# Reads of the rotated keys moved from SyncE's to GpSimd's DMA queue, and a sum of squares moved from GpSimd to VectorE

## The chip, the cores and the metric

The kernel runs on one core of a Trainium2 chip. The metric is device time in microseconds (us); the time before is the median of three runs, 2591.28 us (2590.07 to 2592.25). Engines are called as in the profile: PE is TensorE's matmul, PEld its weight load, DVE VectorE, ACT ScalarE, POOL GpSimd, SP SyncE. A trailing q (SPq, ACTq, POOLq) means the engine's instruction queue, from which DMAs are issued.

## The reference

One encoder layer is applied to a prompt of 512 tokens and a sample of 256, with model width 2048, in float32:

```python
h = rmsnorm(x, ln_mix_g); z = h @ w_in        # columns: fourier 1024 | q 1024 | k 256 | v 256
of = fourier_mix(zf, w_fourier)               # 2-D DFT per group of 128 channels, a 128x128 map
q, k = apply_rope(q), apply_rope(k)           # 16 query heads, 4 key heads, head_dim 64
oa = window_attention(q, k, v, attn_sink)     # +-128 tokens, blocks of 128 queries, a sink logit
x = x + concat(rmsnorm(of), rmsnorm(oa)) @ w_out
x = x + square(relu(rmsnorm(x) @ w_up)) @ w_down     # 8192 wide
y = rmsnorm(x, ln_final_g)
```

## The kernel before, in words

Both requests are handled as one block of T = 768 tokens, six row tiles of 128. Each float32 operand of a product is split in a high part (ACT copies it to the matmul type) and a low part (DVE subtracts), and a product is the sum of three matmuls: high by high, high by low, low by high.

The stages are: row norms, transposes of x and the values (to about 57 us); the Fourier columns of `w_in` by a seven-product scheme (`product7`, L256, to 174 us); the remaining columns of `w_in`, with the Fourier groups and the rotation beside them (L788 to L824, 174 to 378 us); attention together with the first half of the output projection (L1065 to L1080, 378 to about 584 us); the second half with the first residual (L1415 to L1426, to 731 us); the up projection (L1193, to 1665 us); the down projection (L1628, to the end). PE's instructions run in the order of the code all through.

**The columns stage.** `n_in` = 20 pieces, each 1024 rows of `w_in` by 256 columns; four pieces make a column pair. The order of pairs is `cols` (L747): the keys (columns 2048 on), then the queries of groups 2, 0, 1 and 3. Each piece is loaded on SP (`piece_load`, L763, by `wload`, L77, into two `raw` buffers), split by ACT (L69) and DVE (L70), and multiplied on PE (L802). Halfway through and at the end of a pair's fourth piece ACT copies the finished half out of PSUM into the tile `zs` (L815). Pairs 0 and 1 go to DRAM and are read again by `load_z` (L678); pairs 2 to 4 keep their tile, and pairs 2 and 3 use the same single buffer (`z_tile`, L674).

The rotation of a pair is done in three parts of 256 tokens. `cross` (L687) multiplies the swapped halves by the sine on POOL; `turned` (L694, L696) multiplies by the cosine and adds on DVE; `parts` makes the high part on ACT (L706 for keys, L709 for queries) and the low part in place on DVE (L707, L710), and stores both to DRAM on ACT's DMA queue (L704): `kh` and `kl` for keys, `qh` and `ql` for queries. A query's high part lies in one of two `qs` buffers until its store has landed; the low part lies in `zs`.

**The reads that the change moves.** `load_k(i)`, i = 0 to 3, reads the rotated keys back into SBUF in the layout of the score product: 0 and 1 read the high parts into the lower and upper 64 partitions of `kdh`, 2 and 3 the low parts into those of `kdl` (L719). In DRAM the rows are ordered (d h), so that each of 64 partitions takes four rows of 768 floats that lie one after another. Each read moves 768 KB.

What runs beside the products is registered with `after(piece, fn)` (L734) and called when the code reaches that piece (L820 to L824). `load_k(i)` is registered at 14.5 + i (L755), `cross` of the pairs 0, 2, 3, 1 at 10.5, 11.5, 15, 16.5 and half a piece later. Up to piece 18 this order of calls isn't the order on the engines: the framework's scheduler orders SP, ACT, DVE and POOL itself. From piece 19 to the end of attention all engines keep the order of the code (L791).

**Attention** (L1004 to L1080). There are 24 units, six query blocks by four key groups. `load_q` (L730) reads a unit's queries on SP; `qk` (L848) makes the scores, first with `kdl`, then with `kdh`; `row_max` (L863, DVE), `exps` (L878, ACT), `normalize` (L893, POOL), `trans` (L905, PE), the split of the transposed weights (L908, L909) and `pv` (L924) follow. Each call stands in a list of events with a due time in units of the output projection's steps (`at`, `later`, L992 to L997), and `run_events` (L999) emits what is due after each step of `proj_slot` (L1038).

**The squares that the change moves.** `load_oa(m)` (L956) reads a finished row tile of attention outputs from DRAM (L965) in two halves of 128x512, splits them for the projection, and then makes the sums of squares for the group norm: `squares` has ACT square both halves in place (L972) and POOL add one to the other (L973); `reduce` (L976, DVE) sums over the four columns of blocks into `sr`. The two calls are 1.2 steps apart (`t_sq` 6.7, `t_red` 7.9, L989). It is called for m = 0 to 4 in attention, between 463 and 586 us, and for m = 5 in the second half of the projection, at 609 us, where it uses buffers of another tile (`cx`). `row_factors` (L1364) turns `sr` into the factor by a matmul with ones (L1367) and a power on POOL (L101).

Of the kernel before, what the change touches and what calls it, by code (L numbers as in the profile page):

```python
# [15 lines left out]
ALU = mybir.AluOpType  # L16
# [15 lines left out]
NKV = 4  # L32
# [8 lines left out]
def hybrid_encoder(ctx: ExitStack, tc: tile.TileContext, a: dict):  # L41
    nc = tc.nc
    ctx.enter_context(tc.manual_schedule(engines={mybir.EngineType.PE}))

    def f32(ap):
        return ap.bitcast(F32)
# [19 lines left out]
    def split(hi, lo, src, scale=None):  # L66

        if scale is None:
            nc.scalar.activation(hi, src, AF.Copy)  # L69
            nc.vector.tensor_tensor(out=lo, in0=src, in1=f32(hi), op=ALU.subtract)  # L70
        else:
            nc.scalar.activation(hi, src, AF.Copy, scale=scale)
            nc.vector.scalar_tensor_tensor(
                out=lo, in0=src, scalar=scale, in1=f32(hi), op0=ALU.mult, op1=ALU.subtract
            )
# [41 lines left out]
    kr_d = [dpool.tile([2 * P, T], F32, tag=f"k{c}", name=f"k{c}") for c in "hl"]  # L117
# [35 lines left out]
    raws = {}  # L153
# [44 lines left out]
    with ExitStack() as ph:  # L198
# [456 lines left out]
        kt = {}  # L655
# [60 lines left out]

        def load_k(i):
            h = slice(i % 2 * HD, (i % 2 + 1) * HD)
            nc.sync.dma_start(f32(kt["kdh" if i < 2 else "kdl"][h]), kr_d[i // 2][:].rearrange("(d h) t -> d h t", h=NKV))  # L719

        units = [(b, g) for b in range(NM) for g in range(NKV)]
        state = {}
# [32 lines left out]
        for i in range(4):  # L755
            after(14.5 + i, lambda i=i: load_k(i))
# [72 lines left out]
    op = out_ctx.enter_context(tc.tile_pool(name="op", bufs=1, reuse_waits="tile"))  # L829
# [3 lines left out]
    mask, sink, kdh, kdl = (kt[c] for c in ("mask", "sink", "kdh", "kdl"))  # L833
# [116 lines left out]
    def oa_tiles(m):  # L950

        oa[m] = [
            op.tile([P, 8, P], F32R, tag=f"of{c}{m - 1}", name=f"oa{c}{m}") for c in "hl"
        ] + [op.tile([P, P], F32, tag=f"sr{m}", name="sr")]

    def load_oa(m, when=lambda dt, fn: fn(), spare=None):  # L956

        oa_tiles(m)
        oh, ol, sr = oa[m]
        if spare is None:  # L960
            raws = [op.tile([P, 4, P], F32, tag="oar", name="oar", bufs=2)[:] for _ in range(2)]
        else:
            raws = spare
        for i, raw in enumerate(raws):
            nc.sync.dma_start(raw, oa_d[m][i * 512 : (i + 1) * 512, :].rearrange("(k p) t -> p k t", p=P))  # L965

        def parts_of(i):
            split(oh[:, 4 * i : 4 * i + 4, :], ol[:, 4 * i : 4 * i + 4, :], raws[i])

        def squares():  # L970
            for raw in raws:
                nc.scalar.activation(raw, raw, AF.Square)  # L972
            nc.gpsimd.tensor_tensor(out=raws[1], in0=raws[1], in1=raws[0], op=ALU.add)  # L973

        def reduce():
            nc.vector.tensor_reduce(out=sr[:], in_=raws[1].rearrange("p k t -> p t k"), op=ALU.add, axis=AX.X)  # L976

        when(t_oa0, lambda: parts_of(0))
        when(t_oa1, lambda: parts_of(1))
        when(max(t_sq, t_oa0, t_oa1), squares)  # L980
        when(max(t_red, t_sq, t_oa0, t_oa1), reduce)
# [22 lines left out]
    for u in range(len(units)):  # L1004
        t = pace * u + t_first
# [806 lines left out]
```

## Time and profile before

| what | value |
|---|---|
| time, median of 3 runs | 2591.28 us (2590.07 to 2592.25) |
| the profiled execution's own time | 2589.57 us |
| its span in the trace | 2587.7 us |
| granted TensorE clock | 0.999 |
| busy: PE, DVE, ACT, POOL | 2576.2, 1812.2, 1124.0, 257.8 us |
| DMA: mean rate over the span | 188 GB/s |
| DMA share of 16 engines: SP's queue, ACT's, POOL's | 39.3%, 11.7%, 5.8% |
| `load_k`, four issues on SP | at 324.14, 333.58, 339.67, 344.04 us |
| first use of `kdl` and `kdh` on PE | 378.0 us |
| L973 on POOL, six of them | 1.28 to 1.29 us each |

All rows but the first are of one profiled execution. Its time is the span plus 1.9 us around it. Times within the trace are microseconds from the start of the span. [...] In the rows of the timeline, the brackets hold the idle time of the engine just before the instruction and what ended it; "sem" waits of a queue aren't counted as busy.

### The profile page before, as it was taken

The page shows a single profiled execution, that of the slowest core. Times are in us where ns is not written, and L with a number is a line of the kernel's source. Part 1 is how long each engine was busy: PE and PEld are TensorE (multiplying, and loading weights), DVE is VectorE, ACT ScalarE, POOL GpSimd, SP SyncE. Part 2 cuts the span into 40 slices and gives each one's busy share as a digit, 9 for nine tenths or more (in the row PEclk, how much of TensorE's full clock was granted, in tenths as well). Part 3 has the DMA queues.
Part 4 walks back from the last instruction along what each step waited for, and adds up shares of the span by engine and source line. Part 5 has one row for each costly group of instructions (what it writes and reads, how often), then busy time and mean ns, then how long its engine had stood idle before and what let it go on. Part 6 is the DMA issues. An engine that isn't in the chain of part 4 may idle for free.

```text
span 2587.7 us, 34958 instructions
## 1 busy us (share of the span) xinstructions
PE 2576.2 (100%) x13580; PEld 2358.4 (91%) x13580; DVE 1812.2 (70%) x2216; ACT 1124.0 (43%) x1574; POOL 257.8 (10%) x359
## 2 busy tenths in 40 slices
PE   9999999999999999999999999999999999999998
PEld 9999998888899999999999999988888888888887
DVE  7966568777555656555877877667776765777687
ACT  6545437674333333333444544433333333333335
POOL 1001332233201011000000000110000000000000
PEclk9999999999999999999999999999999999999999
DMA  7963385345664445456666666675543662555364
GB/s 252 311 226 113 127 240 181 117 135 193 223 193 157 163 160 186 161 190 238 213 214 232 229 215 208 248 301 178 182 156 111 220 232 82 179 179 164 96 209 155
DMA packets 268999, 489.55 MB, mean 189 GB/s; under 512 B 19568, under 2 KB 164000, under 8 KB 267424
## 3 DMA queue, kind: packets, MB, share of 16 engines
q1 hardware_dynamic: 197328, 321.26, 39.3%
q10 hardware_dynamic: 58688, 115.18, 11.7%
q0 software_dynamic: 12816, 50.87, 5.8%
q8 instruction: 107, 1.75, 0.3%
q14 instruction: 60, 0.49, 0.1%
HBM read 360.35 MB, written 126.88 MB: 188 GB/s over the span
## 4 chain that ended last, share of the span: by engine, by line
PE 98%; DVE 1%; DMA 1%; issue 0%; ACT 0%; DVEq 0%; SPq 0%; POOLq 0%; POOL 0%; ACTq 0%
PE pu L1193 36%; PE pd L1628 35%; PE pm L1046 9%; PE pz L802 6%; PE p L268 5%; PE pv L391 1%; PE o L924 1%; PE s L848 1%; PE t L905 1%; PE pe L630 0%; PE pa L609 0%; PE ptx L137 0%; DMA raw<-in_w_in 0%; PE pt L137 0%; DMA qs<-ql 0%; PE pz L630 0%
## 5 line engine op out<-in xcount | busy, mean ns | idle before, releaser
L1193 PE MATMUL pu<-xf,wh 128*128 128x384 f32 x3072 | 780.1, 334 | 0.0
L1193 PEld LDWEIGHTS pu<-xf,wh 128*128 128x128 f32 x3072 | 554.0, 188 | 1.5 <-ACT o L1211 1.1
L1628 PE MATMUL pd<-wl,sh 128*128 128x512 f32 x1332 | 517.8, 389 | 0.0
L1628 PE MATMUL pd<-wh,sh 128*128 128x512 f32 x1332 | 517.8, 389 | 0.0
L1628 PE MATMUL pd<-wh,sl 128*128 128x512 f32 x1332 | 517.6, 389 | 0.0
L1193 PE MATMUL pu<-xf,wl 128*128 128x384 f32 x1536 | 513.2, 334 | 0.0
L1605 ACT ACTIVATE wh<-rd 128x1024 fp32r<-128x1024 f32 x200 | 202.4, 1054 | 522.2 <-PE pd L1628 421.8
L1615 DVE TENSOR_TENSOR wl<-rd,wh 128x1024 fp32r<-128x1024 f32 x200 | 236.1, 1221 | 226.3 <-ACT wh L1605 225.5
L1173 ACT ACTIVATE wh<-ur 128x1024 fp32r<-128x1024 f32 x160 | 170.0, 1063 | 382.7 <-PE pu L1193 216.8
L1628 PEld LDWEIGHTS pd<-wh,sh 128*128 128x128 f32 x1332 | 250.0, 188 | 51.9
L1628 PEld LDWEIGHTS pd<-wl,sh 128*128 128x128 f32 x1332 | 250.0, 188 | 51.9
L1628 PEld LDWEIGHTS pd<-wh,sl 128*128 128x128 f32 x1332 | 249.9, 188 | 51.8 <-DVE sl L1616 0.3
L1193 PEld LDWEIGHTS pu<-xf,wl 128*128 128x128 f32 x1536 | 288.3, 188 | 0.0
L1179 DVE TENSOR_TENSOR wl<-ur,wh 128x1024 fp32r<-128x1024 f32 x160 | 195.4, 1221 | 75.4 <-ACT wh L1173 75.4
L1214 DVE TENSOR_TENSOR o<-pu,o 128x768 f32<-128x768 f32 x160 | 152.8, 955 | 123.3 <-PE pu L1193 115.1
L1598 DVE TENSOR_TENSOR rd<-rd 128x1024 f32<-128x1024 f32 x112 | 131.7, 1217 | 0.0
L1193 PE MATMUL pu<-xs,wh 128*128 128x384 f32 x512 | 129.8, 334 | 0.0
L1173 ACT ACTIVATE wh<-sx 128x1024 fp32r<-128x1024 f32 x64 | 67.9, 1062 | 130.4 <-PE pu L1193 101.9
L268 PE MATMUL p<-xs,wh 128*128 128x384 f32 x448 | 113.8, 334 | 0.0
L1616 DVE TENSOR_TENSOR sl<-sr,sh 128x768 fp32r<-128x768 f32 x111 | 105.5, 950 | 0.0
L1179 DVE TENSOR_TENSOR wl<-sx,wh 128x1024 fp32r<-128x1024 f32 x64 | 78.1, 1222 | 24.1 <-ACT wh L1173 23.9
L1193 PEld LDWEIGHTS pu<-xs,wh 128*128 128x128 f32 x512 | 92.4, 188 | 0.0
(279 smaller groups left out, 3921.9 us busy)
## 6 DMA issues: line engine op xcount, KB each, us to landing
rd<-in_w_down SPq DMA_DIRECT2D x176, 512.0 KB, 5.2
ur<-in_w_up SPq DMA_DIRECT2D x128, 512.0 KB, 3.9
sr<-sd SPq DMA_DIRECT2D x95, 384.0 KB, 5.4
pd<-o ACTq DMA_DIRECT2D x60, 384.0 KB, 2.3
o<-pd POOLq DMA_DIRECT2D x60, 384.0 KB, 6.0
sd<-sm ACTq DMA_DIRECT2D x60, 384.0 KB, 2.8
raw<-in_w_in SPq DMA_DIRECT2D x38, 512.0 KB, 6.0
raw<-in_w_out SPq DMA_DIRECT2D x32, 512.0 KB, 4.5
```

What stands on the lines that cost most here:

```text
L268: nc.tensor.matmul(ps7[bank, g, r][:, :HALF], l[:, i, r * P : (r + 1) * P], x[:, o, 4 * e + i, :], start=(opens and e == 0 and i == 0 and ...
L802: nc.tensor.matmul(ps[c][s][:, :HALF], w[:, i, cs], whole[j // 2][s][o][:, 4 * (j % 2) + i, :], start=first and n == 0, stop=stop and n == 2,)
L1046: nc.tensor.matmul(ps, l(k), w[:, k % 2, :], start=(k == 0 and n == 0), stop=(k == 7 and n == 2))
L1173: nc.scalar.activation(wh[:], raw[:], AF.Copy)
L1179: nc.vector.tensor_tensor(out=wl[:], in0=raw[:], in1=f32(wh[:]), op=ALU.subtract)
L1193: nc.tensor.matmul(ps[:, t, :HALF], w[:, i, t * P : (t + 1) * P], xb[:, o, i, :], start=(s == first_of[bank] and i == 0 and n == 0), stop= ...
L1214: nc.vector.tensor_tensor(out=o, in0=src, in1=o, op=ALU.add)
L1598: add = lambda x, y, op: nc.vector.tensor_tensor(out=x[:], in0=x[:], in1=y[:], op=op)
L1605: nc.scalar.activation(wh[:], t[:], AF.Copy)
L1615: nc.vector.tensor_tensor(out=wl[:], in0=t[:], in1=f32(wh[:]), op=ALU.subtract)
L1616: nc.vector.tensor_tensor(out=sl[:], in0=sr[:], in1=f32(sh[:]), op=ALU.subtract)
L1628: nc.tensor.matmul(o, l[:, q, ts], w[:, ns], start=(j == j0 and (q, t) == (0, 0)), stop=(j == j1 and (q, t) == (1, 2)),)
```

## The change

The four reads of rotated keys are issued by POOL instead of SP, at the same places of the code. The sum of the two squared halves is made by DVE instead of POOL, at the same due time. Buffers, layouts, due times and arithmetic stay as they are.

```diff
         def load_k(i):
             h = slice(i % 2 * HD, (i % 2 + 1) * HD)
-            nc.sync.dma_start(f32(kt["kdh" if i < 2 else "kdl"][h]), kr_d[i // 2][:].rearrange("(d h) t -> d h t", h=NKV))
+            nc.gpsimd.dma_start(f32(kt["kdh" if i < 2 else "kdl"][h]), kr_d[i // 2][:].rearrange("(d h) t -> d h t", h=NKV))
...
         def squares():
             for raw in raws:
                 nc.scalar.activation(raw, raw, AF.Square)
-            nc.gpsimd.tensor_tensor(out=raws[1], in0=raws[1], in1=raws[0], op=ALU.add)
+            nc.vector.tensor_tensor(out=raws[1], in0=raws[1], in1=raws[0], op=ALU.add)
```

## The prediction, made before the change was run

> **What bounds the kernel now.** I read the page from the top: the span, the engines' busy times, the chain that ended last.
>
> ```profile
> span 2587.7 us, 34958 instructions
> PE 2576.2 (100%) x13580; PEld 2358.4 (91%) x13580; DVE 1812.2 (70%) x2216; ACT 1124.0 (43%) x1574; POOL 257.8 (10%) x359
> PE 98%; DVE 1%; DMA 1%; issue 0%; ACT 0%; DVEq 0%; SPq 0%; POOLq 0%; POOL 0%; ACTq 0%
> ```
>
> The chain is PE from end to end, so an edit matters only where it makes PE wait, or ends a wait. How much waiting there is to end, the busy times by stretch show (columns: stretch, its length, PE busy and then the other engines).
>
> ```profile
> 0.00:64.70 64.70, 61.95 (x467) 59.41 (x468) 49.65 (x72) 42.54 (x61) 12.48 (x23) 1.00 0.70 252
> 370.00:400.00 30.00, 29.86 (x159) 25.75 (x158) 24.43 (x66) 17.34 (x39) 4.60 (x4) 1.00 0.73 225
> 400.00:440.00 40.00, 39.61 (x207) 33.51 (x206) 32.99 (x100) 31.36 (x73) 11.11 (x20) 1.00 0.64 196
> 2000.00:2587.00 587.00, 579.49 (x2568) 480.12 (x2567) 427.43 (x414) 216.14 (x270) 6.03 (x6) 1.00 0.52 169
> sum 2587.00, PE 2576.21 PEld 2358.40 DVE 1812.23 ACT 1123.97 POOL 257.78; mean PE 128.81 PEld 117.92 DVE 90.61 ACT 56.20 POOL 12.89
> ```
>
> PE is idle for 2587.00 - 2576.21 = 10.79 us. The first row holds 2.75 of them, the last 7.51 (start and tail, which the edit doesn't reach), and the two rows between, where attention begins, 0.14 + 0.39 = **0.53 us**. That is all that an edit here can win as long as the order elsewhere stays; what it can lose has no such bound.
>
> So I looked for the place near the moved reads where PE comes closest to waiting. These rows are the timeline of SP, POOL, ACT and the weight loads (columns: start, duration, what; in brackets the idle time before it and who ended it).
>
> ```profile
> 324.14 0.53 SPq L719 DMA_DIRECT2D kdh<-kh  x1
> 333.58 1.22 SPq L719 DMA_DIRECT2D kdh<-kh  x1
> 339.67 0.51 SPq L719 DMA_DIRECT2D kdl<-kl  x1
> 344.04 0.47 SPq L719 DMA_DIRECT2D kdl<-kl  x1
> ...
> 320.57 6.65 POOL L687 TENSOR_TENSOR zy<-zs,sinr 128x256 f32<-128x256 f32 x4 [1.99 <-DVE zs L696]
> 344.50 0.73 POOL L687 TENSOR_TENSOR zy<-zs,sinr 128x256 f32<-128x256 f32 x1 [17.27 <-ACT zs L815]
> ...
> 333.29 0.63 ACT L709 ACTIVATE zh<-zs 128x512 fp32r<-128x512 f32 x1 [4.01 <-DMA qh<-zh]
> 333.95 0.37 ACTq L704 DMA_DIRECT2D qh<-zh  x1
> 334.68 0.37 ACTq L704 DMA_DIRECT2D ql<-zs  x1
> ...
> 339.50 2.05 ACT L69 ACTIVATE wh<-raw 128x1024 fp32r<-128x1024 f32 x1 [2.31 <-DMA raw<-in_w_in]
> 343.88 0.86 ACT L815 COPY zs<-pz 128x384 f32<-128x384 f32 x2 [2.33 <-DMA ql<-zs]
> 344.42 0.19 PEld L802 LDWEIGHTS pz<-xf,wh 128*128 128x128 f32 x1 [0.17 <-ACT zs L815]
> ```
>
> Here is a point with no slack. At 343.88 ACT copies the first half of a column pair (the 1280 columns) out of PSUM, and it was late: the tile it copies into still fed a query store (ql, issued at 334.68) that ACT saw land only then, 9.2 us after its issue. PE needs that bank at 344.42 and waits 0.17 us for the copy. So a microsecond more on that store is a microsecond on the kernel. Before it, ACT at 333.29 waited 4.01 us for an earlier query store (qh). Both are late because of what the DMA engines do between 324 and 344, and the moved reads are a large part of that.
>
> **What the moved reads weigh.** DMA packets by queue in four stretches (q1 is SP's queue, q10 ACT's; packets, MB, share of the 16 engines): 339.8 to 341.2, 345.2 to 347.0, 330 to 333.
>
> ```profile
> q1 hardware_dynamic: 21, 0.26, 82.3%
> q10 hardware_dynamic: 22, 0.02, 8.9%
> ...
> q1 hardware_dynamic: 31, 0.38, 102.7%
> ...
> q10 hardware_dynamic: 1078, 1.04, 101.8%
> ...
> q0 software_dynamic: 12816, 50.87, 5.8%
> ```
>
> (The last row is POOL's queue, from the page, over the whole span.) A read of keys goes in packets of 0.26 MB / 21 = 12.4 KB; 768 KB are 64 of them. Alone they go at 31 / 1.8 us = 17.2 packets a microsecond, 3.7 us a read. The query stores alone go at 1078 / 3 us = 359 packets a microsecond, of 1 KB. In the first two rows both queues have work, and they take turns: 21 packets against 22. While a read of keys runs, a store gets 16 packets a microsecond instead of 359: it stands nearly still. In this kernel SP's order spreads the four reads, and before 344 only two of them have run; the other two run where nothing waits.
>
> **The change, part by part.**
>
> *Moved reads.* Four issues leave SP: 0.53 + 1.22 + 0.51 + 0.47 us of a queue that waits for free buffers, worth nothing. They join POOL. The rows of an issue on POOL, and of the landing of small DMAs from there:
>
> ```profile
> L1697 POOL DMA_DIRECT2D acc<-x x24: 537/537/542, 1671.8 to 1698.5; - x24
> x<-xhl POOLq DMA_DIRECT2D x56, 192.0 KB, 2.4
> ```
>
> Four issues are 4 x 0.54 = 2.1 us of POOL. POOL ends its four products at 320.57 + 6.65 = 327.2 and then has nothing for 17.27 us, so this time is covered; if the issues fell between products instead, the rotation would be at most 2.1 us later. What is queued on POOL between the reads decides the rest. On SP weight loads stood between them, each waiting for a buffer; on POOL there is nothing ready but the reads themselves. The high parts that the first two read had landed by 324.14, when SP issued the first; the low parts follow within a few microseconds. So I expect all four back to back from 327.2 to 329.4, with data from about 329 (2.4 us to land 192 KB, less 0.5 us of data). They then hold every engine for 4 x 3.7 = 14.9 us, to 344 or later.
>
> What this does to the copy at 343.88: before it now lie four reads of keys where two lay, 2 x 3.7 = 7.4 us more. Against that stands engine time that was free; the DMA share (the column before the last) of these stretches gives it:
>
> ```profile
> 328.00:332.00 4.00, 4.00 (x25) 4.00 (x24) 4.00 (x7) 0.63 (x1) 0.00 (x0) 1.00 0.87 248
> 332.00:336.00 4.00, 4.00 (x25) 4.00 (x24) 1.11 (x2) 1.49 (x2) 0.00 (x0) 1.00 0.94 291
> ```
>
> 0.13 x 4 + 0.06 x 4 = 0.8 us. The query stores come last in this, since they take turns with packets twelve times their size and the second group of them (333.95, 334.68) can't be issued before the first has landed (the 4.01 us wait). 7.4 - 0.8 = **+6.6 us** on that store, and with no slack +6.6 us on PE. Nothing returns it: PE is busy without a gap from there to 370. Lower end: the reads start 2 to 3 us sooner, between POOL's products, or only three go early: +3. Upper end: the weight load that ACT splits ahead of the copy (339.50, 2.05 us) is held up as well and its split falls behind the store's landing: +8.7.
>
> [...]
>
> *Squares.* One sum of 128x512 per row tile, six in all, goes from POOL to DVE. Rows: the sum on POOL, an operation of that size and with two SBUF inputs on DVE, what the next step waited for, and ACT's squares and their neighbours at the first tile.
>
> ```profile
> L973 POOL TENSOR_TENSOR oar<-oar x5: 1284/1287/1292, 464.1 to 583.4; 128x512 f32<-128x512 f32 x5
> L70 DVE TENSOR_TENSOR oal<-oar,oah 128x512 fp32r<-128x512 f32 x10 | 7.4, 738 | 1.9 <-ACT oah L69 1.9
> DVE sr L976 <- POOL oar L973: 2.7, 3, 1.6
> 462.90 1.14 ACT L972 ACTIVATE oar<-oar 128x512 f32<-128x512 f32 x2
> 464.45 0.62 DVE L863 CUSTOM_DVE_ANT_0 p<-s,mask,sink 128x384 f32<-128x384 f32 x1 [1.42 <-PE t L905]
> 455.00:585.00 130.00, 96.48 (x302) 1.00 0.39 121
> ```
>
> It takes 1.29 us six times from POOL and puts 0.74 us six times, 4.4 us, on a DVE that is busy 96.48 of 130 us; the reduce behind it no longer waits for POOL (2.7 us). The new wait is DVE for ACT's second square: at the first tile that ends at 464.04, so the sum runs to 464.8 and the mask-and-maximum behind it (464.45) starts some 0.3 us late; the exponentials and PE's later transposes wait for that, and PE shows no idle time in this stretch. I cost it at 0; without that cover it is 4.4 us.
>
> **Sum.** +6.6 and 0. Against the profiled execution: 2587.7 + 1.9 around it = 2589.57 becomes 2596.2. The median of the runs shown is 1.7 us higher (2591.28), so I forecast **2597.9 us** (+0.25%), its own range 2594 to 2600.
>
> **Rivals.**
>
> *The stores get through (not slower).* If the reads leave POOL in smaller packets, or POOL spaces them about as SP did, stores pass sooner. The page's row for POOL's queue speaks for it: 50.87 MB / 12816 = 4.0 KB a packet on average. With 4 KB packets the stores get three turns where they had one; the first group (1024 packets) is through by about 346 and the second 2 us later, +4 us; spaced as now, +0. I take +2: 2593.3. [...] Against it: most DMAs of that queue have no longer rows to send (192 KB over 128 partitions, in the row of landings above, are 1.5 KB each), so the mean says little of a row of 12 KB.
>
> *The reads come late.* If POOL keeps the order of the code, the last reads stand behind the products of the fourth pair:
>
> ```profile
> 363.05 1.94 POOL L687 TENSOR_TENSOR zy<-zs,sinr 128x256 f32<-128x256 f32 x2 [1.54 <-DVE zs L696]
> L848 PE MATMUL s<-kdl,qs x96: 274/281/421, 378.0 to 573.6; 128*128 128x256 f32 x64, 128*128 128x384 f32 x32
> DMA to landing us min/median/max: 8.0/10.0/10.9
> 375.09 0.86 ACT L815 COPY zs<-pz 128x384 f32<-128x384 f32 x2 [2.52 <-DMA ql<-zs]
> ```
>
> The last read is then issued at 365 and lands (8.0 to 10.9 us on SP) at 373 to 376, in time for the first use at 378.0, but up to two reads, 7.4 us, run among the query stores that the next copies out of PSUM wait for (last row). That copy ends at 375.95, 2.1 us before PE turns to attention at 378.0, so up to 7.4 - 2.1 = 5.3 us would show; I take about half, +3: 2594.3. Against it: POOL is idle for 17 us with the reads ready.
>
> *Faster.* If no read of keys ran between 334 and 344 and none hurt later, the copy would come after its split, at 341.6, and 0.17 us of PE's wait goes; with all of the 0.53 us above it is 2590.4, no measurable gain. More than 0.2% could come only from another order of the loads elsewhere.
>
> **Chances.** Forecast 0.55, stores get through 0.28, late 0.10, faster 0.07. The bound is 0.2%, 5.2 us, about what a measurement of this kernel can tell from no change. Of the forecast's cases 85% lie over it, of the late ones half, of the first rival a tenth: slower 0.47 + 0.05 + 0.03 = 0.55, faster 0.07 kept whole, same the rest, 0.38. The range runs from 2590.0 (the reads spaced as now, nothing won) to 2602 (the upper end, +8.7, and 2 us for a late start).
>
> **What would show it.** Four issues in a row on POOL near 327; 12 KB packets on q0 without a break to about 344; the wait of ACT at L709 growing from 4 us to 10 or more; the L815 copy near 350 and an idle stretch of 6 to 7 us on PE ahead of it, the kernel's only new one; POOL without L973, and DVE's sums at about 0.7 us with no idle time on PE. It is wrong if that copy stays near 344, if q0's packets are small, or if new idle time stands somewhere else.

## The result, and the profile after

| | before | after |
|---|---|---|
| median of 6 runs | 2591.44 us (2590.07 to 2592.25) | 2602.18 us (2601.50 to 2604.14) |
| ratio, 95% interval | | 1.0043 [1.0032, 1.0053] |
| profiled execution, its span | 2589.57, 2587.7 us | 2604.14, 2602.3 us |

The change costs 10.7 us by the medians; the forecast was 6.6 us more, and the result lies 0.2 us above the upper end of its range (2602). The profiled executions are before's fastest run and after's slowest, so their spans differ by more, 14.6 us. The trace is read here for where the time goes, the medians for how much.

The page of after, the rows that answer to those of before:

```profile
span 2602.3 us, 34963 instructions
PE 2578.8 (99%) x13580; PEld 2361.3 (91%) x13580; DVE 1814.8 (70%) x2222; ACT 1123.5 (43%) x1574; POOL 253.8 (10%) x357
PE 95%; DVE 2%; DMA 2%; ACT 0%; issue 0%; POOL 0%; POOLq 0%; DVEq 0%; ACTq 0%; SPq 0%
```

PE executes the same 13580 matmuls and is busy 2.6 us longer; the rest is idle time. Busy times by stretch (stretch, length, PE busy, then the other engines; the third number from the end is the granted clock) show where. The first row is of before, the others are of after:

```profile
345.00:370.00 25.00, 25.00 (x145) 24.95 (x145) 17.46 (x25) 7.16 (x10) 11.53 (x12) 1.00 0.70 199
...
345.00:370.00 25.00, 14.79 (x69) 14.70 (x70) 12.03 (x12) 9.18 (x10) 9.65 (x8) 0.73 0.51 160
370.00:400.00 30.00, 29.95 (x168) 28.32 (x167) 21.25 (x38) 11.31 (x20) 8.52 (x9) 1.00 0.67 214
400.00:440.00 40.00, 39.26 (x202) 32.40 (x201) 34.09 (x111) 28.97 (x74) 5.96 (x12) 1.00 0.59 187
455.00:585.00 130.00, 130.00 (x697) 110.78 (x696) 98.06 (x312) 91.39 (x230) 35.02 (x61) 1.00 0.42 129
```

One stretch holds most of it: between 345 and 370 PE is idle 10.2 us, where it had no idle time before, and the clock there is 0.73 on average. The other rows shown are as before to within half a microsecond; in the last one, where the sums of squares now run on DVE, PE has no idle time. The timelines of POOL, ACT, ACT's queue and PE around it:

```profile
327.15 1.13 POOL L719 DMA_DIRECT2D kdh<-kh  x2
328.34 1.02 POOL L719 DMA_DIRECT2D kdl<-kl  x2
...
349.14 0.63 ACT L709 ACTIVATE zh<-zs 128x512 fp32r<-128x512 f32 x1 [19.88 <-DMA ql<-zs]
350.53 0.37 ACTq L704 DMA_DIRECT2D ql<-zs  x1
351.00 3.83 ACT L69 ACTIVATE wh<-raw 128x1024 fp32r<-128x1024 f32 x2 [1.23 <-DMA raw<-in_w_in]
354.61 0.92 ACT L815 COPY zs<-pz 128x384 f32<-128x384 f32 x2
...
355.21 1.71 PE L802 MATMUL pz<-xf,wh 128*128 128x384 f32 x4 [10.92 <-ACT zs L815]
```

These are the links of the forecast's chain. The four reads leave POOL one after another. ACT stands 19.9 us in L709 (4.0 before) for the first query stores; the last store is issued at 350.53 (334.68 before); two splits follow, and the copy comes at 354.61, 10.7 us later than before. PE waits 10.9 us for it. The packets by queue between 336 and 344 in after (packets, MB, share of the engines) show why:

```profile
q0 software_dynamic: 143, 1.38, 69.1%
q1 hardware_dynamic: 138, 0.42, 24.2%
q10 hardware_dynamic: 140, 0.14, 9.6%
```

Three queues take turns, packet by packet: POOL's (q0) with 12 KB (112 of its 143 packets; the other 31 have 4 B), SP's (q1) with 3 KB on average, ACT's (q10) with 1 KB. A store gets 17.5 packets a microsecond, where it had 359 alone in the kernel before.

### The profile page after: what moved, and what is told of

It is laid out like the page before. It is cut to its first block, busy times and chain, and to the rows that moved or that the text cites. A ratio compares the mean times of both kernels' runs of the same rounds, so it can differ in the third digit from the quotient of the medians.

```text
span 2602.3 us, 34963 instructions
## 1 busy us (share of the span) xinstructions
PE 2578.8 (99%) x13580; PEld 2361.3 (91%) x13580; DVE 1814.8 (70%) x2222; ACT 1123.5 (43%) x1574; POOL 253.8 (10%) x357
## 4 chain that ended last, share of the span: by engine, by line
PE 95%; DVE 2%; DMA 2%; ACT 0%; issue 0%; POOL 0%; POOLq 0%; DVEq 0%; ACTq 0%; SPq 0%
PE pu L1193 36%; PE pd L1628 35%; PE pm L1046 9%; PE pz L802 5%; PE p L268 4%; PE pv L391 1%; PE o L924 1%; PE s L848 1%; DMA ql<-zs 1%; PE t L905 1%; DMA raw<-in_w_in 1%; PE pe L630 0%; PE pa L609 0%; PE ptx L137 0%; PE pt L137 0%
```

## The experiments

All times are medians; "over before" is against runs of the kernel before on the same chip (their medians lay between 2589.6 and 2591.1 us). "First copy" and "second copy" are the two at L815 for the fourth column pair (columns 1280 on), which free the halves of PSUM that PE needs next.

### The two parts of the change apart

`e1_reads_only` is the kernel before with L719 on `nc.gpsimd`; `e2_squares_only` has L973 on `nc.vector`.

> Only the reads of the rotated keys move to POOL's queue; the squares' sums stay on POOL. My theory: the whole loss comes from the reads, so 2601 to 2603 us (+10 us on before), the copy at L815 near 354 and PE idle near 10 us ahead of it. Rival (part of the loss comes from VectorE's sums): 2597 to 2600 us.

Measured: 2602.45 us, ratio 1.0039 [1.0026, 1.0053]; first copy at 353.5, PE idle 9.4 us ahead of it. The reads cost the whole.

> Only the sums of the squares move to VectorE; the reads stay on SP. My theory: the 4.4 us of sums lie beside PE's work, so no change, 2590 to 2592.5 us, PE without idle time between 455 and 585. Rival (VectorE's wait for ScalarE's second square holds up the maximum and so the exponentials): 1 to 4 us slower, with idle time on PE in that stretch.

Measured: 2589.76 us, ratio 0.9993 [0.9985, 1.0002]: nothing. Of the profile of this run, the sums and the stretch in which five of the six run:

```profile
L973 DVE TENSOR_TENSOR oar<-oar x5: 680/692/693, 465.6 to 582.1; 128x512 f32<-128x512 f32 x5
455.00:585.00 130.00, 130.00 (x692) 110.42 (x692) 99.53 (x308) 93.77 (x231) 37.51 (x64) 1.00 0.40 122
```

Each sum takes 0.69 us, and PE is busy without a gap.

### How many reads, and how large their packets

`e3_three_reads` puts the fourth read back on SP. `e9_three_in_all` makes it on SP at piece 10, from other data. `e5_small_packets` cuts each read in two halves of its columns:

```diff
-            nc.gpsimd.dma_start(f32(kt[...][h]), kr_d[i // 2][:].rearrange("(d h) t -> d h t", h=NKV))
+            [nc.gpsimd.dma_start(f32(kt[...][h])[:, :, ts], kr_d[i // 2][:].rearrange("(d h) t -> d h t", h=NKV)[:, :, ts]) for ts in (slice(0, HALF), slice(HALF, T))]
```

> As the changed kernel, but the fourth read stays on SP. My theory (each further read ahead of the stores costs its own time): one read too many instead of two, the copy at L815 3 to 5 us late, PE idle 3 to 5 us, 2594 to 2598 us. Rival (it is the bunched issue on a queue of its own, not the number of reads): the loss stays nearly whole, over 2600 us.

> The changed kernel, but only three of the four reads are made there; the fourth (64 partitions of the low parts) is replaced by a read of the same size of other data some 30 us earlier, so the scores are wrong. My theory (each read ahead of the stores costs its own time): the stores end some 4 us sooner, the copy near 350, PE idle 5 to 6 us, 2596 to 2599 us. Rival (as in the run with the fourth read on SP, the number makes little difference): 2600 us or more.

Measured: 2600.27 us (1.0032 [1.0021, 1.0043]) and 2600.30 us (1.0033 [1.002, 1.0045]), both outside my theory's range and inside the rivals'. Neither settles it. In the first, SP issued the fourth read at 345.16, and it still ran ahead of the last store: the copy was at 353.06. In the second the reads started at 329.99, 2.8 us later than in the changed kernel, behind products of POOL that the trace has waiting for the replacement read.

> As the changed kernel, but each read is made in two halves of its columns, so that a row of a packet is 1.5 KB instead of 12 KB; same bytes, same queue, same start. My theory (the stores take turns with packets, and stand still because a packet of the reads is twelve times theirs): with 1.5 KB packets a store gets nearly half of the engines' time, the copy at L815 is at most 2 us late, 2591 to 2595 us. Rival (the four reads together are simply 3 MB in front of the stores, whatever their packets): 2599 to 2603 us.

Measured: 2601.42 us (1.0036 [1.0024, 1.0048]); my expectation failed, and the rival's range holds the time. ACT's timeline of this run, and then the packets of POOL's and ACT's queue between 338 and 344:

```profile
336.18 0.63 ACT L709 ACTIVATE zh<-zs 128x512 fp32r<-128x512 f32 x1 [6.53 <-DMA qh<-zh]
347.56 2.00 ACT L69 ACTIVATE wh<-raw 128x1024 fp32r<-128x1024 f32 x1 [7.53 <-DMA raw<-in_w_in]
352.86 0.86 ACT L815 COPY zs<-pz 128x384 f32<-128x384 f32 x2 [3.30 <-DMA ql<-zs]
```

```profile
q0 software_dynamic: 318, 1.11, 67.3%
q10 hardware_dynamic: 321, 0.31, 17.2%
```

The turns are confirmed: packets of 1.11 MB / 318 = 3.5 KB on average (not the 1.5 KB that I had counted on), stores at 321 / 6 = 53 a microsecond instead of 17.5, and the wait at L709 down from 19.9 to 6.5 us. But the copy is at 352.86 all the same. The stores and the weight load behind them go in packets of 1 KB (0.31 MB / 321, and on SP's queue 0.33 MB / 321 in the same 6 us), by the thousand, and even at 53 a microsecond they aren't through before the reads are. Here packet size decided who moved first; the engines' time, which the reads take either way (67.3% of 6 us for 1.11 MB, 3.6 us a MB; in the changed kernel 69.1% of 8 us for 1.38 MB, 4.0 us a MB), decided when all were done.

### Taking the waits away one by one

In `e7_own_tiles` neither L709 nor the copy waits for a query store; in `e14_third_buffer` only L709 is freed.

```diff
-            zt[pair] = (zo["p"] if pair in (2, 3) else kt["kp"]).tile(...)
+            zt[pair] = (zo["p"] if pair in (1, 2) else kt["kp"]).tile(...)
-            hi = kt["kp"].tile(..., tag="zy" if pair == len(cols) - 1 else "qs", ...)
+            hi = kt["kp"].tile(..., tag="zy" if pair == len(cols) - 1 or (pair, s) == (2, 2) else "qs", ...)
-        for pair, t, ahead in (..., (1, 16.5, 12)):
+        for pair, t, ahead in (..., (1, 16.5, 15)):
```

The fourth pair takes the tile that the keys had, and the pair read back from DRAM that of the third, later. (`e14_third_buffer` has the second edit alone.)

> The changed kernel, reads as there, but the third pair's copies (L815) go to another tile than the one that the second pair's query stores still read, and the third high half has a buffer of its own, so that neither L815 nor L709 waits for a query store. If the stores are what the copy waits for, as I predicted: copy near 344, PE idle under 1 us, 2590.5 to 2594 us. Rival (the weight load that starves beside the reads and lands near 351, with two splits of ScalarE queued ahead of the copy, holds it just as long): copy at 350 or later, PE idle 6 us or more, 2599 to 2602.5 us.

> The changed kernel, but the third high half of the second pair has a buffer of its own, so L709 doesn't wait for the first query stores; the copy still goes to the tile that the last of them reads. Theory (ScalarE stands 20 us in L709, and the last stores and two weight splits of 1.9 us each can begin only after it; this is what my sum left out): first split near 342, copy near 350, PE idle near 6 us, 2598.5 to 2601 us. Rival (the landing of the last store holds the copy, whenever it is issued): copy at 353 or later, 2601.5 to 2603 us.

Measured: 2599.80 us (1.0032 [1.002, 1.0043]) and 2602.01 us (1.0043 [1.0028, 1.0059]). Both rivals won. With tiles of their own:

```profile
348.49 2.00 ACT L69 ACTIVATE wh<-raw 128x1024 fp32r<-128x1024 f32 x1 [4.33 <-DMA raw<-in_w_in]
350.29 0.89 ACT L815 COPY zs<-pz 128x384 f32<-128x384 f32 x2
```

No store is waited for, but the weight load of a later piece, starved in the same way, lands at 348.5, and ACT has its split ahead of the copy. With only L709 freed, the copy (353.77) waits for the store as before.

### The clock

PE's granted clock is halved during the wait and stays so after it (the last section has the rows). `e4_busy_wait` fills the wait with products whose sums are thrown away; `busy_wait(n, w)` makes n of them, of 128x384:

```diff
-            wh, wl = in_w.pop(piece)
+            wh, wl = in_w.pop(piece); piece != 16 or busy_wait(52, wh)
```

> The changed kernel with 52 products of 128x384 more (their sums are thrown away) on PE right ahead of the one that waits for L815: 52 x 0.16 us = 8.3 us of work inside a wait of 9 to 11 us. Theory of the clock (PE's granted clock is halved some 3 us into the idle stretch and stays so for 6 us after it, which costs 3 us that my sum didn't hold): the clock stays at 1.0 and the kernel takes 2598.5 to 2600.5 us, 2 to 3.5 us less than the changed kernel although it does more. Rival (the halved clock in the rows has no price, the whole loss is the wait): 2601.5 to 2603 us, and more if the products come on top.

Measured: 2604.02 us (1.0046 [1.0031, 1.0061]). The 52 products took 9.18 us, not the 8.3 counted on. The clock stayed at 1.0 through that wait, and attention began at 389.8, 1.5 us earlier than in the changed kernel, of which 0.5 us are an earlier first copy. So some 1 us of price shows there, in one profile. But ACT's instructions stand in another order, and PE waited 2.2 us for ACT in attention, so the whole time doesn't show what the clock costs. So two more runs, on `e7_own_tiles`, whose edits differ in nothing but n = 6 or 24:

> The kernel with tiles of their own (PE's wait there 5.9 us) and 6 products of 128x384 more ahead of the waiting one (1 us; their sums are thrown away). The other half of a pair with the run of 24 products: all other instructions stand in the same order in both. PE still stands idle some 5 us, so the clock is halved there and for some 5 us after, as in the run without products: 2599 to 2602 us by either theory.

> As the run with 6 products, but 24 of them (4.1 us), which fills the wait to less than the 3 us after which the clock was halved. Theory of the clock: granted clock 1.0 throughout, and 2 to 3 us less than with 6 products although the wait ends at the same moment. Rival (the halved clock has no price): the same time within 0.7 us.

Measured: 2600.16 and 2601.43 us, ratios to before 1.0039 [1.0026, 1.0053] and 1.0044 [1.003, 1.0058]: no gain. Busy times by stretch in the run with 24:

```profile
345.09:350.90 5.81, 4.33 (x26) 4.01 (x25) 1.58 (x2) 2.38 (x3) 0.00 (x0) 1.00 0.83 291
350.90:360.80 9.90, 6.21 (x32) 5.51 (x33) 3.58 (x2) 3.02 (x4) 3.73 (x2) 1.00 0.54 185
360.80:364.20 3.40, 3.40 (x13) 3.40 (x12) 2.15 (x4) 0.00 (x0) 2.52 (x3) 0.51 0.50 158
```

PE went on at full clock at 350.9, ran 3.7 us ahead of the second copy, whose weights were as late as ever, and stood there (9.90 - 6.21). The time that the clock takes was covered by the next wait, which itself cost a stretch of half clock (last row). The pair isn't quite clean: with 24 products the reads also started 1.05 us later (328.48 against 327.43). With that taken off there is still no gain, so my theory of a price of 3 us falls for this kernel; a smaller price isn't excluded.

### When the reads run

All but `e15_two_and_two` leave the four reads on POOL's queue. VectorE first writes one column of a read's target from a tile that isn't there yet, so the read waits for it; the read then overwrites the column.

```diff
-            h = slice(i % 2 * HD, (i % 2 + 1) * HD)
+            h = slice(i % 2 * HD, (i % 2 + 1) * HD); i % 2 or nc.vector.tensor_copy(kt["kdh" if i < 2 else "kdl"][:, 0, 0:1], zt[3][:, 0, 0:1])
```

That is `e8_late_reads`, whose target waits for the first copy. `e17_three_early` and `e18_two_early` do it for the fourth read, or for the last two, alone; `e19_behind_first` waits for the tile that L709 fills; `e20_spaced` leaves the first read free, the second waits for L709, the last two for the two copies, and the reads are registered half a piece apart instead of a whole one. `e15_two_and_two` has no such write, but the last two reads on SP.

> The changed kernel, but the reads can't start before the first copy at L815: VectorE first writes one column of each key tile from the tile that the copy fills (overwritten by the read). Reads on POOL's queue all the same. My theory (what costs is that the reads run ahead of that copy, not which queue issues them): copy at 343 to 345, PE idle under 1 us there, 2590 to 2594 us. Rival (the reads then stand among the stores of the fourth pair, as in the rival of the prediction): copy at 344, but idle time of 2 to 5 us nearer to 378, 2594 to 2598 us.

> The changed kernel, three reads as there, the fourth (same queue) held back till the first copy at L815 by a one-column write of VectorE. All four are made. If each read ahead of the copy costs its own engine time (3.5 to 4.7 us): copy at 350 to 351, PE idle 5.5 to 7 us, 2596.5 to 2599.5 us. Rival (the number hardly matters, what counts is that a row of reads starts at 327 on a queue of its own): 2600 us or more.

> As the run before, but only two reads early and two held back. By engine time this is what the kernel before had ahead of the copy, except that the two run back to back: copy at 344 to 348, PE idle 0 to 3.5 us, 2590.5 to 2595 us. Rival (the early row of reads as such): 2597 us or more.

> The first two reads on POOL's queue, the last two on SP's where they stood before. If only the number of reads ahead of the last store counts: SP's order puts the third at 340 to 345, so two or three are ahead: copy at 344 to 350, 2591 to 2598 us. Rival (any read on POOL's queue costs the whole): 2600 us or more.

> The changed kernel, but the reads on POOL can't start before L709 has made the third high half (VectorE first writes a column of each key tile from it, overwritten by the read), so the first group of query stores passes ahead of them; three reads then go in a row, the fourth stands behind a product of POOL that waits for the copy. Theory (reads ahead of the first group delay also what ScalarE has queued behind L709: the second group and two splits; with three reads all ahead of it the copy was at 350.3): L709 at 333 to 336, copy at 345.5 to 348.5, 2592 to 2598 us. Rival (only the engine time ahead of the last store counts, wherever the reads stand): copy at 350 or later, 2599 us or more.

> All four reads on POOL's queue, but spaced about as SP spaced them: the first free, the second behind L709's third high half, the last two behind the copies at L815 (VectorE writes a column of the read's target first; overwritten). Theory (what costs is a row of reads without a gap, in which whatever small transfer PE needs next stands still: the stores in the changed kernel, a weight load in the run with the reads behind the first stores): copy at 341 to 345, PE idle under 1.5 us there, 2590 to 2594.5 us. Rival (reads on POOL's queue cost even when spaced): 2597 us or more.

Measured ("in a row" counts the reads that follow each other without a gap; idle time of PE at the two copies):

| run | reads in a row | first copy | second copy | PE idle | time | over before, ratio |
|---|---|---|---|---|---|---|
| `e8_late_reads` | 1, 1, 1, 1 | 340.5 | 346.0 | 0 | 2592.43 | +1.5, 1.0003 [0.9994, 1.0012] |
| `e20_spaced` | 1, 1, 2 | 343.7 | 349.4 | 1.1 | 2595.12 | +4.2, 1.0012 [1.0003, 1.0022] |
| `e15_two_and_two` | 2, 1, 1 | 349.4 | 356.2 | 5.7 | 2597.21 | +6.6, 1.0025 [1.0015, 1.0034] |
| `e18_two_early` | 2, 2 | 347.2 | 353.0 | 3.8 | 2598.70 | +8.1, 1.0029 [1.0018, 1.0041] |
| `e17_three_early` | 3, 1 | 350.3 | 356.2 | 6.2 | 2600.53 | +9.9, 1.0038 [1.0024, 1.0052] |
| the changed kernel | 4 | 354.6 | 360.5 | 10.9 | 2602.18 | +10.7, 1.0043 [1.0032, 1.0053] |
| `e19_behind_first` | 4, behind the first stores | 341.1 | 358.3 | 9.3 | 2602.86 | +13.2, 1.0047 [1.003, 1.0064] |

By their times `e18_two_early` and `e17_three_early` went with the rivals, by their first copies with the theory. The queue isn't the cause: with all four reads on POOL, but one at a time between POOL's products, the loss is gone. POOL's timeline and ACT's of `e8_late_reads`:

```profile
343.36 0.62 POOL L719 DMA_DIRECT2D kdh<-kh  x1
350.60 0.57 POOL L719 DMA_DIRECT2D kdh<-kh  x1
355.63 0.57 POOL L719 DMA_DIRECT2D kdl<-kl  x1
362.69 0.57 POOL L719 DMA_DIRECT2D kdl<-kl  x1
...
340.47 0.92 ACT L815 COPY zs<-pz 128x384 f32<-128x384 f32 x2
```

Two, three and four reads ahead of the first copy put it at 347.2, 350.3 and 354.6: 3.1 to 4.3 us for one more, which is about a read's own 3.7. But two in a row (347.2) are worse than two with a gap between them, as in the kernel before (343.9) and in `e20_spaced` (343.7). The run that I expected to gain from the stores' passing first shows what the gap is for. ACT, then PE, of `e19_behind_first`:

```profile
334.83 0.63 ACT L709 ACTIVATE zh<-zs 128x512 fp32r<-128x512 f32 x1 [4.66 <-DMA ql<-zs]
341.07 0.86 ACT L815 COPY zs<-pz 128x384 f32<-128x384 f32 x2
356.49 2.00 ACT L69 ACTIVATE wh<-raw 128x1024 fp32r<-128x1024 f32 x1 [14.56 <-DMA raw<-in_w_in]
358.30 0.89 ACT L815 COPY zs<-pz 128x384 f32<-128x384 f32 x2
...
358.87 1.70 PE L802 MATMUL pz<-xf,wh 128*128 128x384 f32 x4 [9.34 <-ACT zs L815]
```

The stores are through and the first copy is in time, so the fourth read follows the three without a gap, and then the next weight load starves for 14.6 us instead, its split is late, and the second copy holds PE for 9.3 us. My expectation failed by the wrong wait; the rival's 2599 us or more came true, but not for its reason, since the store's copy was early. `e20_spaced` shows the rest: with gaps both copies are nearly in time (1.1 us), and most of what it loses, 2.9 of 4.2 us, it loses near 382, after the two reads that POOL issued in a row at 361. That these two are the cause is likely, but not shown. POOL's timeline:

```profile
361.27 1.08 POOL L719 DMA_DIRECT2D kdl<-kl  x2 [2.08 <-issue]
```

PE's waits there (us in total, times, longest):

```profile
PE s L848 <- DMA qs<-ql: 2.9, 1, 2.9
```

The times of these runs hold more than the copies: the extra writes can also move neighbours in the scheduler's order, and `e18_two_early` waits 1.4 us for query loads at the start of attention. The column of the first copy is read from instructions ahead of these differences; the column of times is only shown to rise with the row's length, not to be made of it alone.

### A version to keep?

`e13_best` is the kernel before with the sums on DVE and the edits of `e7_own_tiles`.

> The kernel before (reads on SP) with the sums on VectorE and the copies in tiles of their own, so that the point without slack has some. If PE's idle time where attention begins (0.5 us) and the small waits of single runs are what is left to win: 2588.5 to 2590.5 us, 0.5 to 2.5 us under the kernel before. Rival (nothing left there): within 0.5 us of the kernel before.

Measured: 2589.50 us against 2589.96, ratio 0.9997 [0.9988, 1.0006]. That is no gain that can be told: with reads spaced as on SP, the point without slack cost nothing that these runs can tell.

## What held of the prediction, and the step that failed

- **PE bound, little to win, much to lose:** right. The best version found is within the interval of the kernel before.
- **The point without slack:** right. The only new idle stretch on PE of more than 0.6 us is ahead of the L815 copy.
- **Four issues in a row, 12 KB packets, stores at a standstill:** right. 327.15 to 329.36 against the forecast 327.2 to 329.4; 17.5 packets a microsecond against the forecast 16. The turns were shown by `e5_small_packets` too.
- **The squares at nothing:** right, 0.69 us each, and 0.9993 [0.9985, 1.0002] alone.
- **The sum, "7.4 - 0.8 = +6.6 us on that store":** the step that failed, in its second term. All ACT stores of the stretch are 1904 packets in either kernel; the packets by queue from 326 till the last of them has landed (before to 344, then after to 353.4):

```profile
q1 hardware_dynamic: 1615, 3.55, 68.2%
q10 hardware_dynamic: 1904, 1.84, 31.8%
```

```profile
q0 software_dynamic: 320, 3.15, 49.1%
q1 hardware_dynamic: 991, 1.49, 21.7%
q10 hardware_dynamic: 1904, 1.84, 21.2%
```

Before, the engines work 100% of 18 us. After, they work 92% of 27.4 us, that is 25.2: 7.2 more, and the forecast said 7.4. But the forecast had free time shrink by 0.8 us, and it grew by 2.2. The engines stand nearly still (17% busy) from 327.4 till the reads' data begins at 328.5; and at the end the last stores run alone, because they can't be issued before ACT has got past L709, so the engines are 61% busy from 350 to 351 and 7% from 352.2 to 353. (If both stretches end with the last packet of the last store, at 343.4 and 353.05, the two figures are 7.9 and 1.8.) That makes the last store 9.4 us late, and not 6.6. The copy is 10.7 us late, since the two splits that ACT had kept behind L709 (3.83 us, to 354.83) end after the store. The forecast's upper end held one such split (2.05 us); two fell behind. The range's top of 2602 held also 2 us for a late start of the reads, and no run shows that term: in the changed kernel their data began at 328.5, against the forecast's 329. Without it the top was 2600, so it is luck that the result lies only 0.2 us above the range.
- **"With no slack +6.6 on that store and +6.6 on PE":** the mechanism was right, the picture too narrow. The store isn't the only thing that stands still. Take its wait away, and a weight load holds the same copy (`e7_own_tiles`, 5.9 us of PE's wait there and 1.7 us at the next copy) or the next (`e19_behind_first`, 9.3 us). What was lost with the move is the gap that SP's order left after each read.
- **"Nothing returns it":** right, and some is added. The first score product moves from 378.0 to 391.3, 13.3 us for a wait of 10.9; PE works at half clock behind the wait, and the other 2.4 are put down to that, though `e4_busy_wait`, at full clock, began attention only 1.5 us sooner. Behind it stand 1.3 us more of small idle times in attention and the tail. That the medians differ by 10.7 us and not by 14.6 may be a longer wait than usual in the profiled execution or a luckier run of before; `e1_reads_only`, with a wait of 9.4 us, has a span of 2600.3. How the 10.7 us of the medians split isn't settled.

```profile
L848 PE MATMUL s<-kdl,qs x96: 275/281/422, 391.3 to 587.5; 128*128 128x256 f32 x64, 128*128 128x384 f32 x32
```

- **The rivals:** the stores didn't get through: POOL's queue sent all four reads in a row, in 256 packets of 12288 B, and smaller ones wouldn't have helped (`e5_small_packets`, 2601.42 us with packets of 3.5 KB). The reads weren't late by themselves, and `e8_late_reads` shows that lateness alone costs next to nothing (+0.03% [-0.06%, +0.12%]); waits like the rival's (1.4 and 2.9 us at the start of attention) stand in the two runs where two late reads go in a row (`e18_two_early`, `e20_spaced`). A slip without effect: the case "faster" adds up to 2591.28 - 0.17 - 0.53 = 2590.6, not 2590.4.

## What to carry to other kernels

A queue whose loads wait for buffers also spaces what is queued between them (here SP's four issues over 19.9 us, 324.14 to 344.04); move those transfers to an idle queue, and they go out in one row (on POOL 2.2 us, 327.15 to 329.36). Count the row's length in engine time against the slack of every small transfer in that stretch, not only of the one that is latest today: when one wait was taken away in `e7_own_tiles`, the next starved transfer, a weight load, stood at the same place and held PE for 5.9 us. And add to the landing of a late store what its engine has queued behind the wait (here two splits, 3.83 us).

## What the runs showed of the hardware

The granted clock in after, by stretches set at its steps:

```profile
344.50:347.53 3.03, 0.00 (x0) 0.00 (x0) 0.00 (x0) 0.00 (x0) 0.00 (x0) 0.99 0.97 240
347.53:361.18 13.65, 5.97 (x19) 5.88 (x20) 5.10 (x4) 7.72 (x8) 2.37 (x2) 0.50 0.58 193
361.18:370.00 8.82, 8.82 (x52) 8.82 (x52) 6.93 (x9) 1.46 (x3) 7.28 (x7) 1.00 0.28 89
```

It falls to half 3.2 us into PE's wait (which begins at 344.29) and is restored only 5.97 us after PE has resumed: 13.65 us at 0.50 in all, against 3.40 us at 0.51 in the run with 24 products. The length of a short wait alone doesn't decide whether it is punished: one of 2.7 us in `e18_two_early` left the clock at 1.0, one of 2.2 us in `e4_busy_wait` was followed by some 3.4 us at half clock (0.53 on average from 393 to 395, 0.61 from 395 to 397). What decides it these runs don't settle. So a wait can cost PE several microseconds at half speed behind it (5.97 us here), though in the pair of runs that tried to win them back on top of `e7_own_tiles` the next wait took their place.
